# Joining two vector steps of a stick-breaking attention, and moving the loads of its output projection behind the last stores of keys

## The chip, the cores and the metric

The kernel runs on one core of one Trainium2 chip. The metric is the device time of one execution in microseconds (us), the median of several runs. The engines are named as the profile names them: PE (matrix multiply) with PEld (its weight loads), DVE (vector), ACT (scalar), POOL (GpSimd), SP (the queue that issues almost all of this kernel's DMAs).

## The reference

One layer of an encoder over 1024 frames of width 1024, in float32:

```python
h = rmsnorm(x, norm1_g)
qa, ka, va, qb, kb, vb = split(h @ w_in)          # 8 heads of 64 in group A, 8 in group B
ya = chunked_attention(qa, ka, va, rel_bias)      # softmax over 9 chunks of 64 keys
yb = stick_breaking_attention(qb, kb, vb)         # below
x = x + concat(rmsnorm(ya), rmsnorm(yb)) @ w_out
x = x + conv_gated_mlp(rmsnorm(x, norm2_g), ...)  # up 2*2816, causal conv of width 3, SiLU gate, down
return rmsnorm(x, final_g)
```

Stick-breaking attention of one head, for queries t and keys s < t, with z the scaled score: `a = exp(log_sigmoid(z) + suffix)`, where `suffix` is the sum of `log_sigmoid(z) - z` over the keys between s and t. In products: a key's weight is sigmoid(z) times the product of (1 - sigmoid(z)) over the keys between it and the query. If c is the running product of (1 - sigmoid(z)), each weight is the difference of two neighbours of c.

## The kernel before

**Stages.** Times from the profile: values and the projections of group B to about 171 us; stage B, the attention of group B, 176 to 329 us; stage A, the attention of group A, about 339 to 488 us; then the two halves of the output projection (`pb`, `pa`), the second norm and the channel mixer to the end. Time runs backwards in the kernel's arrays (frames are reversed), so that "later" keys of a query are a prefix in memory.

**Who sets the order.** The instruction order of every engine is fixed when the program is written, by a planner in the kernel (`Flow`). A piece of work is a `Chain` of steps, each with the engine it occupies (V, S, G, or D for the DMA queue), a cost from a small formula, and an action that emits the instruction. `flow.add` files a chain with the chains that it comes `after`; `flow.work(us)` moves the planner's clock on with the work of PE and emits every step that could have started by then, earliest first; of steps that could start at the same time the one with the smaller ready time plus `due` goes first. `load(kb, do)` costs `kb/260` us of D and lands 2.2 us later in the planner's eyes. The chip's own waits are semaphores on the data, put in by the framework; the planner decides only the order.

**Filler.** PE's order is: the attention's own products, and between them steps of a generator, `filler()`. A filler step is three matmuls of 128x512 and is counted as 0.68 us. First come the seven projections that group A needs (`project_qk`, tiles `q_p`, `k_p`, 112 steps), then the half of the output projection that belongs to group B (`out_b`, `out_part`, tile `pb`, 64 steps). `run(amount)` takes filler at a fixed rate: RATE_B over a head pair of group B, `RATES_A[p]` us over the eight blocks of head pair p of group A. `ready(*chains)` takes filler for as long as the chains it is given aren't done by the planner's clock; where the generator yields None (nothing to give) it stops, and the planner's clock jumps. `Banks.get` hands out a PSUM bank after `ready` on the bank's last users. `need(n)` draws filler until the projections of head pair n have been stored.

**Stage B.** A `BlockB` is a head pair n and a block i of 128 queries, 64 units of one head in all. `scores` makes z in a bank of 1024 columns (`bigs`, two banks), a chain then does the sigmoid on ACT (L979) and the running product on DVE (`tensor_tensor_scan`, L968, out of PSUM into an SBUF tile `acts`), and a second chain the subtraction of neighbours in `acts` (L974; only the 128 columns of the diagonal block, the other blocks use differences of the values `dv` instead). `turn` waits for that (`ready(self.chain[h])`), transposes `acts` on PE (L998, tile `tpb`), and `output` multiplies with the values (L1012). Unit b's scores are written before the turning of unit b-2. The subtraction is a chain of its own with `due = -2`; the bank counts as free (`mine`) after the scan.

**Stage A.** Blocks of 128 queries, for head pairs p = 0..3 (n = 4..7): scores (`sa`, L1062 and L1063), mask and maximum on DVE, exponential on ACT (L1090), transposes (`tpa`, L1122), copies on ACT (L1126), output (`yy`, L1145). For p, the tiles `qa..lb` of n = p + 4 are loaded from DRAM (`load_qk`, L857, twelve DMAs of 256 KB); the tiles of n and n + 2 share their slots.

**The loads of the output projection.** Group B's heads were normalised and stored to DRAM (`spill`, in `finish_b`, chains `spilled`). `prepare_b(i)` loads two tiles `yh[i]`, `yl[i]` (i = 4..7) of 1 MB in all, in two halves g (L1192); they take the places of the normalised input `hh`, `hl`, which `project_qk` reads to its last step. `out_part` needs for half g the tiles i = 4, 5, 6, 7 one after the other, a filler step each. `load_x2(d)` loads the residual (L1227) that a finished part is added to (L1219). The stores of the keys of n = 7 (`qk_kept[7]`, L838) come from the last projection.

The part of `filler` after the projections, and the chain that each half's load is put behind:

```python
            load_x2(0)
            load_x2(1)
            for i in range(4, 8):
                while not spilled[i - 4]:
                    yield None
                prepare_b(i)
...
                last = [yb_chains[i - 1, g]] if i > 4 else [x2_chains[g]]
                yb_chains[i, g] = flow.add(load(512, begin), after=[*spilled[i - 4], *last])
```

Of the kernel before, what the change touches and what calls it, by code (L numbers as in the profile page):

```python
# [39 lines left out]
BACK, BACK_STEP = 1.0, 0.6  # L40
BEHIND_V = {"V": 1.0, "S": 5.0, "D": 7.0}
RATE_B, LEAD_B = 10.0, 4.0
RATES_A, LEAD_A = (11.0, 13.0, 13.0, 13.0), 6.5
LAG = 0.25
START = 8.0
SLACK = 0.6
# [18 lines left out]
def r32(ap):  # L65
    return ap.bitcast(F32)
# [3 lines left out]
def tile_hybrid_block(  # L70
# [44 lines left out]
    def one(tag, name, dt=F32, shape=(P, T), pool=cp):  # L115
        return pool.tile(list(shape), dt, tag=tag, name=name)
# [33 lines left out]
    def rows(g):  # L150
        return slice(g * GW, (g + 1) * GW)

    def mm3(outs, wh, wl, sl, mh, ml, first, last, groups=(0, 1)):
        for i, (w, t) in enumerate(((wh, mh), (wh, ml), (wl, mh))):
            for o, g in zip(outs, groups):
                PE.matmul(  # L156
                    o, w[:, sl], t[:, rows(g)],
                    start=first and i == 0, stop=last and i == 2,
                )

    def cols(k):
        return slice(k * P, (k + 1) * P)
# [30 lines left out]
    def hpair(k, name, tags=None):  # L193
        th, tl = tags or (f"h{k}", f"l{k}")
        return one(th, f"{name}h{k}", F32R), one(tl, f"{name}l{k}", F32R)
# [5 lines left out]
    with tc.tile_pool(name="kp", bufs=2) as kp:  # L201
# [422 lines left out]
        def on_v(n, do, own="V"):  # L624
            return own, n / 960 + 0.075, 0.09, do

        def on_s(n, do):
            return "S", n / 1200 + 0.1, 0.1, do
# [4 lines left out]
        def load(kb, do, us=2.2):  # L633
            return "D", kb / 260, us, do
# [118 lines left out]
        flow, raw_chains = Flow(), {}  # L753
# [28 lines left out]
        def fetch(queue=w_ready, pool=wp, tags=("wh", "wl"), bufs=None):  # L782

            if not w_next:
                return
            if (w_next[0] in LATE_W) != (queue is w_late):
                w_missed.append(1)
                return
            name, t, loaded = w_next
            w_next.clear()  # L790

            def high():
                t["h"] = pool.tile([P, D], F32R, tag=tags[0], name=f"{name}_h", bufs=bufs)
                S.copy(t["h"], t["r"])  # L794

            def low(c, n, eng):
                if not c:
                    t["l"] = pool.tile([P, D], F32R, tag=tags[1], name=f"{name}_l", bufs=bufs)
                c = slice(c, c + n)
                sub(t["l"][:, c], t["r"][:, c], t["h"][:, c], eng)  # L800

            if name == LATE_W[1]:
                rest = [on_v(D, lambda: low(0, D, V), "VL")]
            else:
                rest = [on_g(PIECE, lambda c=c: low(c, PIECE, GP)) for c in range(0, D, PIECE)]
            c = flow.add(on_s(D, high), *rest, after=[loaded], slack=SLACK)
            c.due = DUE
            queue.append((t, c))
            load_next([c])
# [3 lines left out]
        def take(queue=w_ready):  # L813
            t, c = queue.popleft()
            flow.need(c)
            return t["h"], t["l"]
# [10 lines left out]
        qk_kept = {n: [] for n in range(8)}  # L827
# [50 lines left out]
        def project_qk(n):  # L878
            for what in ("q", "k") if n > 4 else ("k",):
                wh, wl = take()  # L880
                outs, mine = [None] * G, [None] * G
                steps = [(g, k) for g in range(G) for k in range(KT)]
                count = [0] * G
                for i, (g, k) in enumerate(steps):
                    if not count[g]:
                        for _ in range(PATIENCE):
                            if pjs.free():
                                break
                            yield None
                        outs[g], mine[g] = pjs.get(f"{what}{n}_p{g}")  # L890
                    count[g] += 1
                    last = count[g] == KT
                    mm3(outs[g : g + 1], wh, wl, cols(k), hh[k], hl[k], count[g] == 1, last, (g,))
                    flow.work(0.68)
                    if i == len(steps) - 1:
                        fetch()
                    if last:
                        mine[g].append(spill_qk(n, what, outs, g))
                    yield 0.68
# [32 lines left out]
        class BlockB:  # L932
# [14 lines left out]
            def scores(self, h):  # L947
                i, nk = self.i, self.nk
                qa, qb, ka, kb, la, lb = [qk_of[self.n][i] for i in range(6)]
                q, k, l = ((qa, ka, la), (qb, kb, lb))[h]  # L950
                z, mine = bigs.get(f"z{self.nm}_{h}")
                w = nk * P

                at, parts = {
                    1: (P, ((0, 2 * P, -P),)), 5: (192, ((192, 320, 0), (GW, 320, 320))),
                }.get(nk, (0, ((0, GW, 0), (GW, w - GW, GW)) if nk > 4 else ((0, w, 0),)))
                for o, n, k0 in parts:
                    ks = slice(i * P + k0, i * P + k0 + n)
                    PE.matmul(z[:, o : o + n], q[:, cols(i)], k[:, ks], start=True, stop=False)
                    PE.matmul(z[:, o : o + n], q[:, cols(i)], l[:, ks], start=False, stop=True)  # L960
                    flow.work(n / 1200 + 0.03)
                z = z[:, at : at + w]
                a = b_acts.pop(0)
                b_acts.append(a)
                self.a[h] = a

                def left():
                    V.tensor_tensor_scan(  # L968
                        out=a[:, :w], data0=z, data1=first[:, :w], initial=1.0, op0=ALU.mult,
                        op1=ALU.max,  # L970
                    )

                def steps():
                    V.tensor_tensor(  # L974
                        out=a[:, : P - 1], in0=a[:, : P - 1], in1=a[:, 1:P], op=ALU.subtract
                    )

                mine.append(flow.add(
                    on_s(w + 75, lambda: S.activation(z, z, AF.Sigmoid, scale=-1.0)),  # L979
                    on_v(2 * w + 100, left),  # L980
                ))
                self.chain[h] = flow.add(on_v(190, steps), after=mine)
                self.chain[h].due = -2.0

            def turn(self, h, mate):

# [166 lines left out]
        rb_of, sq_of, y_chains, x2_chains, yb_chains = {}, {}, {}, {}, {}  # L1153
# [32 lines left out]
        def prepare_b(i):  # L1186
            yh[i], yl[i] = hpair(i, "y")
            for g in range(G):

                def begin(r=rows(g)):  # L1190
                    for t, x in zip(spill[i - 4], (yh[i], yl[i])):
                        nc.sync.dma_start(r32(x[:, r]), t[:, r])  # L1192

                last = [yb_chains[i - 1, g]] if i > 4 else [x2_chains[g]]
                yb_chains[i, g] = flow.add(load(512, begin), after=[*spilled[i - 4], *last])

        def out_part(wh, wl, base, d, g, name):
            o, mine = pjs.get(f"{name}_{d}_{g}")
# [26 lines left out]
        def load_x2(d):  # L1225
            x2[d] = one(X2_TAGS[d], f"x2_{d}")
            x2_chains[d] = flow.add(load(512, lambda: nc.sync.dma_start(x2[d], xT[d])))  # L1227
# [165 lines left out]
        def filler():  # L1393
            for n in PLAIN:
                yield from project_qk(n)
            load_x2(0)
            load_x2(1)
            for i in range(4, 8):
                while not spilled[i - 4]:
                    yield None  # L1400
                prepare_b(i)
            while 4 not in rb_of or any(not c.done or c.t > flow.now for c in rb_of[4][1]):
                yield None
            yield from out_b(EARLY)
            while at["qk"] < 6:
                yield None
            yield from out_b((2,))

        fill = filler()
        done = [0.0]  # L1410

# [34 lines left out]
        spilled, summed = [None] * 4, [None] * 4  # L1446
# [47 lines left out]
        with stage("b"):  # L1494
# [11 lines left out]
            for b in range(len(items) + 3):  # L1506
                cur, h = items[b] if b < len(items) else (None, 0)
# [14 lines left out]
                if ending:  # L1522
# [4 lines left out]
                    yy, mine = meds.get(f"y{pair[0].nm}")  # L1527
# [17 lines left out]
                if 0 <= b - 2 < len(items):  # L1545
                    u, h = items[b - 2]
# [71 lines left out]
        for b in range(len(blocks) + 2):  # L1618
# [24 lines left out]
            if cur and cur.p == 3 and cur.i in (3, 4):  # L1643
                g = cur.i - 3
                ready(last_sum[2, g])
                rn_chains["a", g] = flow_totals(sq_of[0][:, rows(g)], f"na_{g}", rn3[:, 4 * g : 4 * g + 4])
            for h in range(2):
                if cur:
                    cur.scores(h)
                if ending and h == 0 and ending.i % 2:  # L1650
# [4 lines left out]
                    yy, mine = meds.get(f"yy{ending.p}_{ending.i}")  # L1655
# [119 lines left out]
    with stage("ffn"):  # L1775
# [449 lines left out]
        steps = {}  # L2225
# [130 lines left out]
        for f in range(3, NF):  # L2356
            if f + 2 < NF:
                load_up(f + 2)
            left = Left(f + 1) if f + 1 < NF else None
# [138 lines left out]
```

## Time and profile before

| | |
|---|---|
| median of 3 runs (lowest, highest) | 1212.7 us (1212.63, 1214.37) |
| the profiled execution | 1214.88 us, of which 1213.2 us lie between its first and last instruction |
| busy: PE, PEld | 1192.5 us (98%), 985.0 us (81%) |
| busy: DVE, ACT, POOL | 927.6 us (76%), 681.9 us (56%), 157.4 us (13%) |
| granted PE clock | 0.996 of full speed |
| DMA | 166.92 MB, 138 GB/s on average |

Busy time of an engine is the union of its instructions' times; what is left of the span is its idle time, and for each idle stretch the profile names the instruction on another engine (or the DMA) whose end came last before the engine went on. PE is busy nearly throughout, so idle time of PE is what this kernel can still lose or win by its order. A granted clock of 1 in a stretch means that PE was not throttled there.

### The profile page before, as it was taken

Reading aid. Unit: us, or ns where it says so; the run is one execution under the profiler, and the core shown is the slowest. Engines: PE = TensorE matmul, PEld = TensorE weight load, DVE = VectorE, ACT = ScalarE, POOL = GpSimd, SP = SyncE. Lnnn points to the kernel's source line nnn. Section 1 sums busy time; section 2 is a strip of 40 time slices with the busy share of each in tenths; the row PEclk is TensorE's granted clock in tenths of the full one; section 3 lists DMA queues with packets and bytes.
Section 4 is the critical chain, followed back from the end, with each engine's and each line's share of the span. In section 5 each row is a group of like instructions: output and inputs, shape, how many; then the busy total and the mean of one; then the engine's idle time right before and its main releaser. Section 6 shows DMA issues by size and latency. Waiting matters only on the chain.

```text
span 1213.2 us, 17081 instructions
## 1 busy us (share of the span) xinstructions
PE 1192.5 (98%) x6268; PEld 985.0 (81%) x6268; DVE 927.6 (76%) x1383; ACT 681.9 (56%) x1251; POOL 157.4 (13%) x161
## 2 busy tenths in 40 slices
PE   9999999999999899999999999999999999999997
PEld 7788888888888678888878888888888888888886
DVE  7957748878766666459997877768777789979885
ACT  7865336666667766334665555555555555444435
POOL 0001031002211210332000000000000023132035
PEclk9999999999999999999999999999999999999998
DMA  9468686777377841243033222232222295520003
GB/s 331 135 209 264 192 244 182 204 184 196 123 205 188 241 111 53 87 143 120 35 104 105 71 86 89 69 105 70 87 87 70 88 367 239 193 85 1 1 1 139
DMA packets 73793, 166.92 MB, mean 138 GB/s; under 512 B 7783, under 2 KB 23271, under 8 KB 73710
## 3 DMA queue, kind: packets, MB, share of 16 engines
q1 hardware_dynamic: 73566, 165.79, 43.3%
q8 instruction: 49, 0.80, 0.3%
q14 instruction: 34, 0.28, 0.1%
q10 hardware_dynamic: 144, 0.05, 0.0%
HBM read 118.60 MB, written 47.20 MB: 137 GB/s over the span
## 4 chain that ended last, share of the span: by engine, by line
PE 68%; DVE 5%; ACT 2%; DMA 1%; issue 1%; SPq 0%; DVEq 0%; ACTq 0%
PE u_c L1895 9%; PE u_e L1895 9%; PE u_a L1895 9%; PE dz L2411 8%; PE u_b L1895 5%; PE dj L2411 4%; PE dm L2411 4%; PE pb L156 4%; PE pa L156 3%; PE yy L1145 2%; PE tpa L1122 2%; PE k_p L156 2%; PE q_p L156 2%; PE dnl L2331 1%; PE sa L1062 1%; PE sa L1063 1%
## 5 line engine op out<-in xcount | busy, mean ns | idle before, releaser
L968 DVE TENSOR_TENSOR_SCAN acts<-zb,first 128x128 f32<-128x128 f32 (+7 forms) x64 | 85.1, 1348 | 25.2 <-ACT zb L979 25.1
L1919 DVE SCALAR_TENSOR_TENSOR vt<-cv,taps,vt 128x1023 f32<-128x1023 f32 (+1 forms) x44 | 58.2, 1322 | 2.2 <-ACT vt L1913 1.4
L1919 DVE SCALAR_TENSOR_TENSOR gt<-cg,taps,gt 128x1023 f32<-128x1023 f32 (+1 forms) x44 | 56.4, 1281 | 0.9 <-ACT gt L1913 0.2
L1090 ACT ACTIVATE pa<-sa,sta 128x640 f32<-128x640 f32 (+4 forms) x64 | 43.1, 673 | 21.3 <-DVE sta L1081 10.3
L134 POOL TENSOR_TENSOR dx_0wl<-dr,dx_0wh 128x512 fp32r<-128x512 f32 x1 | 1.4, 1370 | 412.4 <-ACT dx_0wh L2162 412.4
L1002 ACT COPY tb<-tpb 128x128 f32<-128x128 f32 (+3 forms) x96 | 43.3, 485 | 16.2 <-PE tpb L998 15.7
L979 ACT ACTIVATE zb<-zb 128x128 f32<-128x128 f32 (+7 forms) x64 | 41.3, 645 | 17.5 <-PE zb L960 17.1
L1913 ACT ACTIVATE gt<-cg,cst,taps 128x1024 f32<-128x1024 f32 x22 | 27.4, 1245 | 37.0 <-DVE cg L1787 37.0
L998 PE MATMUL tpb<-ident,acts 128*128 128x128 f32 x288 | 43.8, 279 | 1.3 <-DVE acts L974 0.8
L1126 ACT COPY pta<-tpa 128x512 f32<-128x512 f32 (+3 forms) x80 | 36.8, 486 | 11.2 <-PE tpa L1122 11.0
L1081 DVE TENSOR_REDUCE sta<-sa 128x1 f32<-128x640 f32 (+4 forms) x64 | 41.9, 655 | 1.2
L998 PEld LDWEIGHTS tpb<-ident,acts 128*128 128x128 f32 x288 | 33.0, 140 | 11.9 <-issue 3.9
L1122 PE MATMUL tpa<-ident,pa 128*128 128x128 f32 x240 | 38.1, 278 | 3.8 <-ACT pta L1126 2.4
L1784 DVE TENSOR_TENSOR up_r<-up_r 128x512 f32<-128x512 f32 x60 | 41.2, 687 | 0.8
L1122 PEld LDWEIGHTS tpa<-ident,pa 128*128 128x128 f32 x240 | 27.6, 140 | 11.9 <-ACT pta L1126 4.8
L1078 DVE TENSOR_TENSOR sa<-sa,bias 128x256 f32<-128x256 f32 (+1 forms) x64 | 26.4, 413 | 11.3 <-PE sa L1063 8.2
L2083 ACT COPY u_b<-u_a 128x512 f32<-128x512 f32 x19 | 10.8, 571 | 38.1 <-PE u_a L1895 38.1
L1145 PE MATMUL yy<-pta,v 128*64 128x256 f32 (+1 forms) x288 | 29.7, 349 | 0.0
L1012 PE MATMUL yb<-tb,dv 128*64 128x128 f32 x448 | 29.5, 273 | 0.0
L1784 DVE TENSOR_TENSOR dr<-dr,dr 128x512 f32<-128x512 f32 x40 | 28.9, 741 | 0.0
L1707 POOL TENSOR_TENSOR n_acc<-n_acc,n_sq 128x384 f32<-128x384 f32 (+2 forms) x23 | 24.1, 1049 | 29.0 <-ACT n_sq L1706 28.3
L134 POOL TENSOR_TENSOR wo_l<-wo_r,wo_h 128x256 fp32r<-128x256 f32 x28 | 19.7, 736 | 62.4 <-ACT wo_h L794 62.4
(1403 smaller groups left out, 4012.5 us busy)
## 6 DMA issues: line engine op xcount, KB each, us to landing
up_r<-in_w_up_dram SPq DMA_DIRECT2D x44, 512.0 KB, 3.6
act<-vt SPq DMA_DIRECT2D x22, 512.0 KB, 2.6
dr<-in_w_dn_dram SPq DMA_DIRECT2D x20, 512.0 KB, 6.8
dr<-act SPq DMA_DIRECT2D x20, 512.0 KB, 7.9
wv<-in_w_v_dram SPq DMA_DIRECT2D x16, 256.0 KB, 5.4
xin<-in_xT_dram SPq DMA_DIRECT2D x16, 256.0 KB, 5.4
row<-in_x_rows_dram SPq DMA_DIRECT2D x16, 256.0 KB, 2.7
raw<-in_w_in_dram SPq DMA_DIRECT2D x8, 512.0 KB, 5.1
```

The costliest lines, as they stand in the source:

```text
L156: PE.matmul(o, w[:, sl], t[:, rows(g)], start=first and i == 0, stop=last and i == 2,)
L968: V.tensor_tensor_scan(out=a[:, :w], data0=z, data1=first[:, :w], initial=1.0, op0=ALU.mult, op1=ALU.max,)
L998: PE.transpose(tp[:, cols(b)], self.a[h][:, cols(b0 + b)], ident)
L1002: mine.append(flow.add(on_s(m * P, lambda o=o, tp=tp: S.copy(o, tp))))
L1081: V.tensor_reduce(out=st[:, h : h + 1], in_=full, axis=AX.XY if nk == 5 else AX.X, op=ALU.max, negate=True,)
L1090: on_s(w + 170, lambda: S.activation(po, full, AF.Exp, bias=st[:, h : h + 1], accum_out=st[:, 2 + h : 3 + h])),
L1122: PE.transpose(tp[:, cols(b)], self.pr[src][:, cols(c)], ident)
L1145: PE.matmul(yy[HS[h], q], v[:, c * P + h * 64 : c * P + (h + 1) * 64], t[:, h], start=j == 0, stop=j == len(parts) - 1, skip_group_check=True,
L1784: eng.tensor_tensor(out=out, in0=a, in1=b, op=ALU.subtract)
L1895: PE.matmul(o, w[:, cols(k)], t, start=start and k == 0 and i == 0, stop=k == 3 and i == 2, skip_group_check=True,)
L1919: V.scalar_tensor_tensor(out=t[:, : T - lag], in0=o[:, lag:], scalar=c1(c + ct), in1=t[:, : T - lag], op0=ALU.mult, op1=ALU.add,)
L2411: PE.matmul(o[m], w[:, cols(m)], t, start=i in (0, 1, 4, 5) and p == ps_[0] and j == 0, stop=p == ps_[-1] and j == 2, skip_group_check=True,)
```

## The change

Three edits.

1. In `BlockB.scores` the scan and the subtraction become one step of one chain, emitted back to back on DVE, with a cost of `2w + 270` elements in place of `2w + 100` and, in a chain of its own, `190`. The chain that `turn` waits for and the chain that frees the bank are now the same: the planner counts the bank as used until the subtraction is done.
2. In `filler`, after the projections, the generator yields None until the stores of group B's last head pair and of the keys of n = 7 have been emitted. Then all four `prepare_b` are called at once, and `load_x2(0)`, `load_x2(1)` after them. A half's load no longer comes after the half before it.
3. `RATES_A` becomes (11, 13, 10, 11).

No instruction is added or removed; the order and the places change.

```diff
-RATES_A, LEAD_A = (11.0, 13.0, 13.0, 13.0), 6.5
+RATES_A, LEAD_A = (11.0, 13.0, 10.0, 11.0), 6.5
...
                         out=a[:, :w], data0=z, data1=first[:, :w], initial=1.0, op0=ALU.mult,
                         op1=ALU.max,
                     )
-
-                def steps():
                     V.tensor_tensor(
                         out=a[:, : P - 1], in0=a[:, : P - 1], in1=a[:, 1:P], op=ALU.subtract
                     )
 
-                mine.append(flow.add(
+                self.chain[h] = flow.add(
                     on_s(w + 75, lambda: S.activation(z, z, AF.Sigmoid, scale=-1.0)),
-                    on_v(2 * w + 100, left),
-                ))
-                self.chain[h] = flow.add(on_v(190, steps), after=mine)
-                self.chain[h].due = -2.0
+                    on_v(2 * w + 70 + 200, left),
+                )
+                mine.append(self.chain[h])
...
-                last = [yb_chains[i - 1, g]] if i > 4 else [x2_chains[g]]
-                yb_chains[i, g] = flow.add(load(512, begin), after=[*spilled[i - 4], *last])
+                yb_chains[i, g] = flow.add(load(512, begin), after=spilled[i - 4])
...
+            while not spilled[3] or not all(c.done for c in (*spilled[3], *qk_kept[7])):
+                yield None
+            for i in range(4, 8):
+                prepare_b(i)
             load_x2(0)
             load_x2(1)
-            for i in range(4, 8):
-                while not spilled[i - 4]:
-                    yield None
-                prepare_b(i)
```

## The prediction

> **What bounds the kernel now.** First the busy times of the page, then the stretches of the stages, then the instructions of PE one by one where PE is idle, then the queue of SP in that stretch.
>
> ```profile
> PE 1192.5 (98%) x6268; PEld 985.0 (81%) x6268; DVE 927.6 (76%) x1383; ACT 681.9 (56%) x1251; POOL 157.4 (13%) x161
> ```
> ```profile
> core 0: us, PE busy (x) PEld busy (x) DVE busy (x) ACT busy (x) POOL busy (x), PEclk, DMA share, GB/s
> 176.00:329.50 153.50, 151.94 (x1255) 126.62 (x1253) 122.43 (x159) 96.71 (x195) 19.97 (x25) 1.00 0.69 183
> 345.00:394.20 49.20, 49.13 (x340) 40.18 (x341) 33.42 (x85) 36.61 (x96) 3.93 (x8) 1.00 0.82 202
> 394.20:406.50 12.30, 9.02 (x70) 6.55 (x68) 7.74 (x19) 9.62 (x24) 3.55 (x6) 1.00 0.99 317
> 406.50:429.00 22.50, 18.84 (x137) 14.16 (x136) 15.39 (x41) 16.09 (x46) 2.86 (x4) 1.00 0.88 200
> 429.00:450.00 21.00, 21.00 (x139) 17.08 (x139) 13.41 (x33) 13.58 (x40) 1.29 (x1) 1.00 0.43 108
> 450.00:488.00 38.00, 37.98 (x265) 31.02 (x264) 26.18 (x65) 26.31 (x69) 5.38 (x7) 1.00 0.12 43
> 488.00:510.70 22.70, 22.70 (x113) 18.59 (x112) 11.24 (x18) 6.64 (x10) 7.18 (x11) 1.00 0.31 102
> ```
>
> PE bounds nearly everything: whatever order the work is in, its 1192.5 us stay, and a change of order can win only idle time. In stage B (first stretch) that is 153.50 - 151.94 = 1.56 us. In stage A it is 3.28 us from 394.2 to 406.5 and 3.66 us from 406.5 to 429, together 6.94, and next to nothing before (0.07) and behind (0.02). So there is one hole, 35 us long. The rows of PE in it, with the last filler step of the projections (`k_p`) and the first of the output projection (`pb`):
>
> ```profile
> 393.95 0.39 PE L156 MATMUL k_p<-hTh,k_l 128*128 128x512 f32 x1
> ...
> 397.29 0.66 PE L1122 MATMUL tpa<-ident,pa 128*128 128x128 f32 x4 [1.82 <-ACT pta L1126]
> ...
> 405.91 0.39 PE L1062 MATMUL sa<-kb,qb 128*128 128x256 f32 x1 [1.03 <-ACT pa L1090]
> ...
> 406.50 0.48 PE L156 MATMUL pb<-yh,wo_h 128*128 128x512 f32 x1
> ...
> 410.54 0.44 PE L1122 MATMUL tpa<-ident,pa 128*128 128x128 f32 x2 [0.28 <-ACT pta L1126]
> ...
> 414.12 0.41 PE L1062 MATMUL sa<-ka,qa 128*128 128x320 f32 x1 [1.34 <-ACT pa L1090]
> ...
> 417.57 0.48 PE L156 MATMUL pb<-yh,wo_h 128*128 128x512 f32 x1
> ...
> 419.79 0.48 PE L156 MATMUL pb<-yh,wo_h 128*128 128x512 f32 x1
> ...
> 428.86 0.44 PE L1122 MATMUL tpa<-ident,pa 128*128 128x128 f32 x2 [1.23 <-DVE yq L1574]
> 429.05 0.48 PE L156 MATMUL pb<-yh,wo_h 128*128 128x512 f32 x1
> ```
>
> The releasers are links of the softmax chain, which are there at all times; elsewhere filler covers them. Here there is none: three single `pb` steps at 406.5, 417.6 and 419.8 in 35 us, and from the fourth, at 429.05, a steady flow and no idle time. The four steps are those that need tiles i = 4, 5, 6 and 7. The queue of SP says why they come so far apart:
>
> ```profile
> 387.78 1.31 SPq L1227 DMA_DIRECT2D x<-in_xT_dram  x2
> ...
> 396.63 0.33 SPq L838 DMA_DIRECT2D k_d<-k_f  x1
> 397.05 0.50 SPq L1192 DMA_DIRECT2D yh<-spill  x1
> ...
> 401.69 0.62 SPq L1192 DMA_DIRECT2D yl<-spill  x1
> 407.80 0.45 SPq L857 DMA_DIRECT2D qa<-q_d  x1
> ...
> 410.79 0.57 SPq L1192 DMA_DIRECT2D yh<-spill  x1
> ...
> 421.27 0.32 SPq L1192 DMA_DIRECT2D yl<-spill  x1
> ...
> 428.30 0.45 SPq L857 DMA_DIRECT2D lb<-k_d  x1
> ```
> ```profile
> SPq L857 <- PE sa L1063: 7.4, 2, 5.4
> ```
>
> Eight of the sixteen loads of `yh`, `yl` go out from 397.05 to 401.69, already behind the last store of keys. The other eight follow from 410.79 to 421.27, because the loads for head pair 3 (`qa`..`lb`) stand between and in front: the first of them waits up to 5.4 us for PE to leave the slot, and SP with it.
>
> **The loads (edit 2).** Nothing is added; what moves is the place of 16 loads of `y` and two of `x2` in SP's queue. The chain from half to half goes, and both `x2` go behind. The loads are filed when the projections end, those of head pair 3 only with its turn, some 14 us later; the planner prefers the one that is ready earlier, so all sixteen stand in front of `qa`. They start where they do now (the keys' store at 396.63 is in front of them already, so the new wait for that store costs nothing; it is hidden because no filler could run before the tiles are there). The planner takes 512/260 = 1.97 us for a half and 2.2 us to land, halves of g = 0 and 1 in turn: tiles 4 to 7 of g = 0 are there 4.2, 8.1, 12.0 and 16.0 us after a start at about 397, so it puts the steps at about 403 (behind the transposes and outputs already due), 406, 410 and 414 in place of 406.5, 417.6, 419.8 and 429. The data would be there: the second eight, 2.1 MB, take 6.6 us at the 317 GB/s of the third stretch and 10.5 us at the 200 of the fourth, so the last are issued by about 412 at the slowest, and the one that the fourth step needs earlier.
>
> From 414 on filler flows. Of the 3.66 us of the fourth stretch, 0.28 (at 410.54) and 1.34 (at 414.12) lie before that, and two steps of 0.69 us (below) fall among them: about 0.6 stays and 3.0 go. Of the 3.28 of the third stretch the 1.82 at 397.29 stays, since no tile is there; of the 1.03 at 405.91 the first step takes about half. Term: -3.5 us. Ends: 0, where the steps fall beside the gaps, and -6.94, where all idle time went. The `x2` loads end about 4 us later than the last `y`; they are first used by the addition behind the fourth step, and the bank it frees is wanted eight steps later: no cost, and if that cover were gone the 2 x 512 KB at 200 GB/s cost 5 us.
>
> What is late next is head pair 3's twelve loads, behind 1 MB of `x2` now.
>
> ```profile
> 447.93 0.39 PE L1062 MATMUL sa<-ka,qa 128*128 128x320 f32 x1
> ```
>
> This is its first use. Today's last load goes out at 428.30; the 1 MB adds 5 us at 200 GB/s, and the 9 us that SP's pause (401.69 to 410.79) leaves unused come back. About 435 against a use at 444 or later: nothing. The Trainium skill, "DMA: Bandwidth & Descriptors", section "Queues, rings and completion order", says that each DMA engine consumes one ring's descriptors in order, which speaks against putting 5 MB in front of the keys; the order of the rows above agrees, and by that rule alone the keys would still be early.
>
> **The rates (edit 3).** Head pairs 2 and 3 get 10 and 11 us of filler for 13 and 13: 5 us move behind stage A, where the filler runs without a gap:
>
> ```profile
> 504.26 2.75 PE pb L156 x12
> ```
>
> That is four steps, 0.69 us each. PE does the same work there, so moving costs nothing unless thinner filler opens gaps. The nearest row is the stretch 345 to 394.2, mostly head pair 0 at 11 us: 0.07 us idle. `ready` also draws filler beyond the rate where a chain is late. Term: +0.3 us; ends 0 and +5 (all that is moved becomes idle time).
>
> **Scan and subtraction (edit 1).** The same 128 instructions of DVE. Rows of the group, and one place where another scan stood between:
>
> ```profile
> L968 DVE TENSOR_TENSOR_SCAN acts<-zb,first x64: 396/1340/2292, 176.7 to 323.0; 128x128 f32<-128x128 f32 x8, 128x1024 f32<-128x1024 f32 x8, 128x256 f32<-128x256 f32 x8, 128x896 f32<-128x896 f32 x8
> L974 DVE TENSOR_TENSOR acts<-acts x64: 257/283/2209, 177.1 to 324.3; 128x127 f32<-128x127 f32 x64
> ```
> ```profile
> 274.27 2.59 DVE L968 TENSOR_TENSOR_SCAN acts<-zb,first 128x768 f32<-128x768 f32 x2
> 276.78 2.18 DVE L974 TENSOR_TENSOR acts<-acts 128x127 f32<-128x127 f32 x2
> ```
> ```profile
> 278.91 0.85 PE L998 MATMUL tpb<-ident,acts 128*128 128x128 f32 x6 [0.64 <-DVE acts L974]
> ...
> 280.22 0.55 PE L998 MATMUL tpb<-ident,acts 128*128 128x128 f32 x3
> ...
> 285.39 0.74 PE L998 MATMUL tpb<-ident,acts 128*128 128x128 f32 x5 [0.19 <-DVE acts L974]
> ```
>
> Two scans, then their two subtractions, and the first unit's transposes wait 0.64 us. Joined, the first subtraction ends a scan earlier and that wait and the 0.19 go: -0.8. The second unit's scan starts 0.28 us later; its transposes (280.22) come 1.26 us after their subtraction ends (276.78 + 2.18 = 278.96), so that is covered; without that cover 32 such pairs cost 32 x 0.28 = 9 us. The bank is really free after the scan (the subtraction doesn't touch it); only the planner holds it 0.28 us longer and puts a filler step earlier instead: +0.3. Term: -0.5; ends -1.56 (all idle time of the stage) and +9, and I stay near the first, because DVE is busy 122.43 of 153.5 us there and PE does not wait for it otherwise. The Trainium skill, "VectorE: DVE Perf Modes", section "Rules for kernel authors", says that fusing chained vector operations gains nothing, only fewer of them do. The median of 283 ns agrees, for DVE's own time; by the rule the term is 0 and the sum -3.2.
>
> **Sum.** -3.5 + 0.3 - 0.5 = -3.7 us. The profiled execution took 1214.88 us (span 1213.2), 2.2 us over the median of 1212.7: 1211.2 for such an execution, 1209.0 for the median.
>
> **Rivals.** What a measurement can tell from no change is about 0.2%, 2.4 us.
>
> *Nothing gained.* The hole is a stretch without filler because the tiles can't be loaded before the projections end; its gaps at 397 and 405 lie before any tile, and if steps fall beside the gaps the term is -1 and the sum -1: 1212. For it: half of the idle time has such a place. Against: the gaps at 414 and 428.86 lie behind the tiles' new times.
>
> *Slower: thin filler.* In head pairs 2 and 3 the 5 us taken away become idle time: -3.5 + 5 - 0.5 = +1, and with no gain from the loads +4.5: 1214 to 1217. It decides once over 3.7 us of the 5 turn idle. For it: without filler the hole has 6.94 us idle in 34.8. Against: the 0.07 above.
>
> *Slower: the second scan.* If the later second scan of a pair is what the turning waits for, it costs up to 9 us, 1217; it decides from 13 of the 32 pairs on. Against: the 1.26 us above.
>
> *Keys late.* If SP's order moves head pair 3's loads past 444, each us counts; at 10 us late 1219. Against: 9 us in hand.
>
> **How the numbers follow.** Forecast 0.55 (1206 to 1210.3; its own range comes from a hole closed by 2.4 to 6.9 us), nothing gained 0.25 (1210.3 to 1215), thin filler 0.10, second scan 0.07, keys 0.03. Faster 0.55, same 0.25, slower 0.20. The range reaches from 1205.5 (hole closed, stage B's idle gone) to 1216 (into the thin filler) and leaves out about 0.15.
>
> **What would show it.** All sixteen `yh`, `yl` loads in one run on SP from 397 to about 410, `qa` behind them; four `pb` steps before 416 and steady ones behind; idle time of PE in the hole down from 6.94 to about 3.4; idle below 1 us in head pairs 2 and 3; more `pb` steps after the last `yy`; no scan between a scan and its subtraction, and PE's waits for `acts` down from 0.8. I am wrong if the `y` loads are split by `qa` again, if PE waits for a DMA at a `pb` step, or if the idle time shows up again between 430 and 485.

## The result, and the profile after

The changed kernel takes 1210.93 us (median of 14 runs), the kernel before in the same session 1212.99 us (14 runs). The ratio is 0.9982, with a 95% interval of 0.9974 to 0.9990: 0.18% faster, about 2.1 us. The forecast was 1209.0, in a range from 1205.5 to 1216.

Executions of one and the same kernel take some 1.4 us longer where their granted clock is 0.995 or 0.996 than where it is 0.997 or 0.998, and two took two to three times as long as all others (one of the changed kernel's 14, 2421 us, and the profiled one of `e_before` below, 3455 us), so times that are set against each other below are medians over executions at 0.997 or 0.998: 1212.9 for the kernel before (59 executions beside the experiments) and 1210.7 for the changed one (9), a difference of 2.2 us. The profiled execution of before had 0.996, that of the changed kernel (1210.40 us, span 1208.7) 0.998.

First the busy times of the changed kernel, and the same stretches as before:

```profile
PE 1189.4 (98%) x6268; PEld 984.7 (81%) x6268; DVE 932.1 (77%) x1383; ACT 682.3 (56%) x1251; POOL 157.1 (13%) x161
```
```profile
core 0: us, PE busy (x) PEld busy (x) DVE busy (x) ACT busy (x) POOL busy (x), PEclk, DMA share, GB/s
176.00:329.50 153.50, 151.37 (x1262) 129.28 (x1261) 126.28 (x158) 98.80 (x198) 20.18 (x25) 1.00 0.69 186
345.00:394.20 49.20, 48.64 (x336) 39.29 (x334) 33.49 (x85) 36.00 (x96) 4.68 (x10) 1.00 0.76 189
394.20:406.50 12.30, 9.70 (x71) 6.98 (x73) 7.88 (x20) 10.31 (x28) 4.07 (x5) 1.00 0.91 297
406.50:429.00 22.50, 21.02 (x150) 17.19 (x147) 16.02 (x41) 15.29 (x41) 1.35 (x2) 1.00 1.04 276
429.00:450.00 21.00, 20.52 (x140) 15.97 (x141) 15.20 (x40) 14.87 (x45) 4.32 (x7) 1.00 0.17 49
450.00:488.00 38.00, 37.88 (x263) 30.47 (x260) 24.77 (x61) 25.26 (x67) 4.09 (x5) 1.00 0.21 76
```

Two things stand out. From 345 to 429 PE is idle for 0.56 + 2.60 + 1.48 = 4.6 us, where it was idle for 0.07 + 3.28 + 3.66 = 7.0 us; behind 429 it is idle for 0.48 + 0.12 = 0.6 us, where there was 0.02. And PE's busy time, of the same 6268 instructions, fell by 3.1 us, which a mere change of order was not supposed to do. In stage B (first stretch) idle time even rose, from 1.56 to 2.13 us.

SP's queue, with the last stores of keys (`k_d`), the first and the last of the sixteen loads, and what follows them:

```profile
394.86 0.33 SPq L838 DMA_DIRECT2D k_d<-k_f  x1
395.28 0.41 SPq L1189 DMA_DIRECT2D yh<-spill  x1
...
404.90 0.32 SPq L1189 DMA_DIRECT2D yl<-spill  x1
405.56 1.01 SPq L1223 DMA_DIRECT2D x<-in_xT_dram  x2
...
407.73 0.45 SPq L857 DMA_DIRECT2D qa<-q_d  x1
...
422.22 0.45 SPq L857 DMA_DIRECT2D lb<-k_d  x1
```

All sixteen stand in one run from 395.28 to 404.90, where before the second eight went out from 410.79 to 421.27. The last load of head pair 3 goes out at 422.22 instead of 428.30. PE in the same place, its idle stretches and the `pb` steps:

```profile
392.18 0.39 PE L156 MATMUL k_p<-hTh,k_l 128*128 128x512 f32 x1
...
395.52 0.66 PE L1119 MATMUL tpa<-ident,pa 128*128 128x128 f32 x4 [1.82 <-ACT pta L1123]
...
402.87 0.47 PE L156 MATMUL pb<-yh,wo_h 128*128 128x512 f32 x1
...
404.14 0.39 PE L1059 MATMUL sa<-kb,qb 128*128 128x256 f32 x1 [0.33 <-ACT pa L1087]
...
405.49 0.38 PE L1059 MATMUL sa<-ka,qa 128*128 128x256 f32 x1 [0.52 <-ACT pa L1087]
...
408.32 0.39 PE L156 MATMUL pb<-yh,wo_h 128*128 128x512 f32 x1
...
412.55 0.41 PE L1059 MATMUL sa<-ka,qa 128*128 128x320 f32 x1 [1.36 <-ACT pa L1087]
...
416.01 0.48 PE L156 MATMUL pb<-yh,wo_h 128*128 128x512 f32 x1
...
416.79 0.39 PE L156 MATMUL pb<-yh,wo_h 128*128 128x512 f32 x1
...
417.48 0.39 PE L156 MATMUL pb<-yh,wo_h 128*128 128x512 f32 x1
```

The hole, from the last `k_p` step to the fourth `pb` step, is 24.6 us long instead of 35.1. Its steps came at 402.9, 408.3, 416.0 and 416.8. No `pb` step waits for a DMA.

### The profile page after: what moved, and what is told of

Read it like the earlier page. It is cut to its first block, busy times and chain, and to the rows that moved or that the text cites. A ratio compares the mean times of both kernels' runs of the same rounds, so it can differ in the third digit from the quotient of the medians.

```text
span 1208.7 us, 17078 instructions
## 1 busy us (share of the span) xinstructions
PE 1189.4 (98%) x6268; PEld 984.7 (81%) x6268; DVE 932.1 (77%) x1383; ACT 682.3 (56%) x1251; POOL 157.1 (13%) x161
## 4 chain that ended last, share of the span: by engine, by line
PE 87%; DVE 8%; ACT 3%; issue 1%; DMA 0%; POOL 0%; DVEq 0%; SPq 0%; ACTq 0%; POOLq 0%
PE u_c L1891 9%; PE u_e L1891 9%; PE u_a L1891 9%; PE dz L2407 8%; PE u_b L1891 5%; PE dj L2407 4%; PE dm L2407 4%; PE pb L156 3%; PE pa L156 3%; PE k_p L156 3%; PE v_x L510 3%; PE q_p L156 2%; PE yy L1142 2%; PE v_y L510 2%; PE tpa L1119 2%; PE tpb L995 2%
```

## The experiments

The theory: the loads close the hole and win most of what is won, the join a little, the rates nothing. The rivals: the gain comes from one edit alone; the edits undo each other; the join costs or wins by the bank and not by its order. The table gives, for each profiled execution, the length in us of the stages on PE, counted from start to start of instructions (B: first `zb` to the first `sa` of stage A; hole as above; rest: to the last `yy` of stage A; tail: to the last `pb`, with the number of its steps; pa: to the last `pa`). "Stages" is the sum of the columns and of the head pairs of stage A ahead of the hole (54.3 to 54.4, but 55.1 in `e_bank`), less that of the kernel before (380.4). "Time" is the difference of the medians at the higher clock, and the last column is the ratio of all runs, the two long ones left out, with its interval.

Five profiles have the same order of PE in stage B, that of before, and there B is 162.8, 162.9, 163.0, 163.4 (`e_tail`) and 163.7 (before itself); the table takes 162.9 for before, near the middle one. With its own 163.7 every other kernel would stand 0.8 lower in "stages", which the times don't bear out.

| kernel | B | hole | rest | tail (steps) | pa | stages | time | ratio |
|---|---|---|---|---|---|---|---|---|
| before | 162.9 (163.66 in its own profile) | 35.10 | 60.38 | 21.06 (28) | 46.57 | 0 | 0 | |
| changed | 161.99 | 24.61 | 69.02 | 21.04 (28) | 46.83 | -2.6 | -2.2 | 0.9982 (0.9974 to 0.9990) |
| e_scan | 162.03 | 35.10 | 60.39 | 21.06 (28) | 46.57 | -0.9 | -1.0 | 0.9989 (0.9980 to 0.9998) |
| e_loads | 162.80 | 24.60 | 72.41 | 16.51 (22) | 48.43 | -1.3 | -1.5 | 0.9986 (0.9977 to 0.9995) |
| e_rates | 162.94 | 35.09 | 60.18 | 22.78 (30) | 46.56 | +1.5 | +2.2 | 1.0013 (1.0004 to 1.0022) |
| e_noscan | 163.00 | 24.62 | 69.05 | 21.04 (28) | 47.05 | -1.3 | -1.3 | 0.9984 (0.9975 to 0.9993) |
| e_bank | 162.59 | 35.08 | 60.41 | 21.08 (28) | 46.66 | +0.5 | +0.5 | 1.0001 (0.9992 to 1.0010) |
| e_join | 162.05 | 24.61 | 69.34 | 21.04 (28) | 46.96 | -2.1 | -1.9 | 0.9984 (0.9975 to 0.9994) |
| e_tail | 163.44 | 35.11 | 64.44 | 16.53 (22) | 49.11 | +2.6 | +2.0 | 1.0013 (1.0004 to 1.0022) |
| e_halves | 161.95 | 17.68 | 77.54 | 16.49 (22) | 48.43 | -4.0 | -4.0 | 0.9963 (0.9951 to 0.9976) |
| e_halves_thin | 161.98 | 17.69 | 75.17 | 18.35 (24) | 46.58 | -6.3 | -6.4 | 0.9942 (0.9929 to 0.9954) |
| e_both | 160.82 | 17.57 | 75.44 | 19.04 (25) | 46.55 | -6.6 | -6.6 | 0.9943 (0.9931 to 0.9956) |
| e_pieces | 160.74 | 17.68 | 75.38 | 18.31 (24) | 46.64 | -7.3 | -7.3 | 0.9944 (0.9931 to 0.9958) |

The sums of stages and the times agree within 0.4 us in all rows but two (`e_rates` 0.7, `e_tail` 0.6): what is won and lost lies in these stages. The second norm and the channel mixer behind them are unchanged code; their 654.7 to 656.3 us go with the clock, 656.0 and more in the four profiles at 0.995 or 0.996 and 655.3 or less in the nine others. In all thirteen the clock is 1 from stage B up to the last 15 us, so the stages of the table are not touched by it.

**The kernel before once more** (no edit), as the measure of what a comparison can tell:

> The kernel before once more, for a second profile. The changed kernel was 2.06 us faster in the medians, but its profiled span is 4.5 us shorter, and 3.35 us of that lie between the first scores of group B and the last product of pa. Theory A (the three edits changed only those stages, the rest is scatter of the profiled execution): the stretch from the first scores to the last pa is 381.1 us again within 0.3, stage B 163.7, and the rest of the span is shorter by about 1 us than in the first profile. Theory B (stage B itself scatters from execution to execution by more than a microsecond, so the 1.67 us that it lost after the change prove nothing): stage B comes out between 162 and 163. Time: 1212.99, ratio 1.000.

Its ratio is 0.9998 (0.9989 to 1.0007): differences under 0.1% can't be told by ratios alone, and the stages in the profile have to tell them. Its profile is of the execution of 3455 us and can't decide what it was taken for, whether stage B scatters. The five profiles above do: it scatters by 0.9 us in the order of before. The PE instructions are the same, and the lengths differ behind one place, where DVE waits for a DMA of `spill`, a store of group B's finished heads:

```profile
231.76 0.75 DVE L1461 SCALAR_TENSOR_TENSOR yb<-y,cst,yb 128x512 fp32r<-128x512 f32 x1 [1.50 <-DMA spill<-yb]
```

That is before. In `e_tail`, `e_noscan`, `e_rates` and `e_loads` the same row waits 1.33, 0.93, 0.68 and 0.46 us, in the order of their B (163.4, 163.0, 162.9, 162.8); from PE's scores at about 233 and 239 on, the stage runs later where the wait was longer (by 0.65 us in before against `e_noscan`). The kernels with the join have no wait in this row, and their B is 161.95 to 162.05 in five profiles (those with POOL's work in pieces, further below, are shorter still).

**Each edit alone, and two together.** `e_scan` is edit 1 alone, `e_loads` edit 2, `e_rates` edit 3 (their parts of the diff above), `e_noscan` edits 2 and 3.

> Edit 1 alone (scan and subtraction as one step). Theory A (joining takes away waits of transposes for their subtraction, which the profile hides partly because a matmul counts as busy for 0.39 us while the next starts after 0.23): stage B about 162.0 us as in the changed kernel against 163.7, the hole in stage A with 6.9 us of idle time as before; in all -1.7 us, 1211.3. Theory B (the gain of stage B is scatter, the rule that fusing gains nothing): stage B 163.7 and 1213.0. Theory C (the bank counted as used for longer costs): over 164.5 in stage B, 1214.

> Edit 2 alone (the loads behind the stores of keys, all at once). Theory A (the hole in stage A lasts as long as the filler lacks its tiles): the hole from the last projection step to the fourth pb step is 25 us long in place of 35, its idle time about 4.6 in place of 6.9, idle time behind it under 0.1 with the full rates; stage B unchanged at 163.7. In all -2.3 us, 1210.7. Theory B (the loads were hidden anyway and the whole gain came from stage B): the hole is shorter, its idle time turns up elsewhere, 1212.5 to 1213.

> Edit 3 alone (less filler in head pairs 2 and 3). Theory A (thinner filler opens small gaps behind the hole): idle time behind the hole about 0.6 in place of 0.02, hole unchanged, more pb steps after the last yy (about 33 in place of 28): +0.5 us, 1213.5. Theory B (filler is drawn on demand, a lower rate only moves it): 1213.0.

> The changed kernel without edit 1 (edits 2 and 3 alone). Theory A (edits 2 and 3 only work together, and edit 1 adds its part of stage B): stage B 162.8, the hole 24.6 us, 28 steps left, pa 46.8; +0.85 on the changed kernel, 1211.8. Theory B (edit 1 has no part in it): 1210.9.

The join is worth about 0.9 us wherever it stands: B is 162.0 with it and 162.8 to 163.7 without, and by time it wins 1.0 on the kernel before (`e_scan`) and 0.8 between `e_noscan` and the changed kernel. The loads alone win 1.3, although the hole closes by the full 10.5 us. Of that, 1.9 us come back in the output projection of group A (pa, 46.57 to 48.43). Its waits, in `e_loads` and (further below) `e_tail`; columns are total, number, longest:

```profile
PE pa L156 <- ACT wo_h L794: 0.7, 1, 0.7
```

PE waits there for the cast of a weight tile (`wo_h`). Filler that is given out earlier is missing behind the last `yy`: 22 steps instead of 28, and the casts for `pa` had run beside these steps. The rates put the six steps back (28) and pa is 47.0 again, but thinner filler lengthens rest and tail by 69.05 + 21.04 - 72.41 - 16.51 = 1.2 us. Edit 3 beside edit 2 is therefore 1.2 - 1.4 = -0.2 by these stages, nothing that the times show. Alone it has no wait to remove (28 steps were enough) and costs 1.5 by the stages and 2.2 in time, more than either theory of its expectation; the other 0.7 lie in none of the stages.

**Is the tail of filler the cover?** If the missing steps are the cause, filler given out earlier must cost the same with the loads of before:

```diff
-RATES_A, LEAD_A = (11.0, 13.0, 13.0, 13.0), 6.5
+RATES_A, LEAD_A = (11.0, 13.0, 13.0, 17.0), 6.5
```

> The kernel before with one rate raised: 17 in place of 13 us of filler in head pair 3, so that about 22 pb steps are left behind the last yy in place of 28. Loads and their order as before. In the run of edit 2 alone, and in that of the halves in another order, 22 steps were left and pa took 48.4 us in place of 46.6, with 0.7 us of PE waiting for the cast of a weight. Theory A (these steps are the cover under which the weights of pa are loaded, cast and split; edit 3 is there to keep them): pa 48.4 us and the same wait, all else as before, +1.8 us, 1214.7. Theory B (the longer pa comes from the moved loads): pa 46.6, 1213.

```profile
PE pa L156 <- ACT wo_h L794: 1.3, 1, 1.3
```

With 22 steps behind the last `yy` the wait is there without any moved load, and pa is 49.1 us. (Of the +2.6 in the table 0.5 is its longer B; rest, tail and pa together cost 2.1.) Moving filler forward is no free move: the last 24 steps or so are the cover of the next weights (24 keep pa at 46.6 in `e_halves_thin`).

**What of the join wins: its order, or the bank that is held longer?** `e_bank` is before with the bank counted as used until the subtraction; `e_join` is the changed kernel with the bank counted as free 0.2 us earlier.

```diff
 # e_bank, on the kernel before
                 self.chain[h].due = -2.0
+                mine[:] = [self.chain[h]]
 # e_join, on the changed kernel; Sooner passes on a chain's state with its time less 0.2
-                mine.append(self.chain[h])
+                mine.append(Sooner(self.chain[h], 0.2))
```

> The kernel before, but a bank of scores counts as free only after the subtraction, which stays a step of its own. In the run of edit 1 alone, stage B took 162.0 us against 162.8 to 162.9 in the two runs without edit 1, and the filler stood in other places: 46 times straight before scores and 7 times before transposes, against 26 and 19. Theory A (the late bank does it: the planner draws filler before the scores, where it gives the subtraction time): about 46 and 7 here too, stage B near 162.0, 1212.0. Theory B (the join does it, by taking other scans out from between): 26 and 19 about as before, stage B 162.8 or longer, 1213.0.

> The changed kernel, but the planner counts a bank of scores as free 0.2 us before the joined step ends, about when the scan itself ends. Theory A (late bank): filler back before the transposes, stage B 162.8, in all +0.8 on the changed kernel, 1211.8. Theory B (join): stage B 162.0, 1210.9.

With the bank alone B is 162.59, 0.2 below the shortest in the order of before, and 0.7 us are lost in the head pairs ahead of the hole (55.06 instead of 54.37). With the bank back, the join keeps B at 162.05. So it is the join. How much of its gain is the wait for `spill` that goes with it, no run separates. But it doesn't win by the waits that the prediction named. The rows of `acts` in the changed kernel (minimum, median and maximum in ns), and stage B of `e_noscan`, whose clock is the same:

```profile
L968 DVE TENSOR_TENSOR_SCAN acts<-zb,first x64: 415/1350/2291, 176.6 to 321.3; 128x128 f32<-128x128 f32 x8, 128x1024 f32<-128x1024 f32 x8, 128x256 f32<-128x256 f32 x8, 128x896 f32<-128x896 f32 x8
L972 DVE TENSOR_TENSOR acts<-acts x64: 290/292/2354, 177.1 to 322.6; 128x127 f32<-128x127 f32 x64
```
```profile
PE tpb L995 <- DVE acts L972: 1.3, 1, 1.3
```
```profile
176.00:329.50 153.50, 152.14 (x1258) 127.20 (x1257) 122.60 (x159) 97.12 (x197) 19.99 (x25) 1.00 0.70 183
```

Three short waits of transposes for `acts` (1.1 us together) became one of 1.3 us, the next scores wait twice for a scan (0.9 us together, none in `e_noscan`), idle time in the stage rose from 1.36 to 2.13, and still the stage is 1.0 us shorter: PE's busy time holds hidden waits. Two matmuls of 512 columns that wait for nothing start 0.23 us apart (391.04 and 391.27 in the trace of the changed kernel), while each has a duration of 0.39: a matmul that comes up to 0.16 us late shows no gap. Counted from start to start, less the smallest interval behind a filler matmul in the stage, transposes right behind a filler step lost about 1.0 us at 19 places in `e_noscan` and lose 0.15 at 7 in the changed kernel, since the joined order puts filler ahead of the scores (46 places for 26) and not ahead of the transposes. The scores behind filler lose in turn, 0.8 us for 0.2, so 0.3 of these two stays as gain. Other successions change in both directions; how the 1.0 us divides further stays open.

The Trainium skill, "Perfetto Trace Analysis", section "Identifying the Most-Contended Engine", says that matmul busy share is no good measure of how close a kernel is to its roofline, because pipelined instructions look smaller in the trace. These runs agree that it is no measure: 2.2 us of busy time went between `e_noscan` (1191.6) and the changed kernel (1189.4), 1.8 of them in stage B, with the same 6268 matmuls and the same clock of 0.998. They don't show it by that reason: a row here is longer (0.39 us) than the step to the next matmul (0.23).

**The loads in the order in which the steps need them.** The planner gives halves 0 and 1 in turn; `out_part` needs the four tiles of half 0 first.

```diff
             for i in range(4, 8):
-                prepare_b(i)
+                prepare_b(i, 0)
             load_x2(0)
             load_x2(1)
+            for i in range(4, 8):
+                prepare_b(i, 1)
```

`e_halves_thin` has RATES_A (11, 13, 8, 11) beside it, so that filler is left behind stage A.

> The changed kernel with the loads in another order: the four halves g = 0 first, then the residuals, then the four halves g = 1. In the changed kernel the hole (last projection step to fourth pb step) is 24.6 us with 4.6 us of idle time, 1.36 of it in one piece, 18 us in. Theory A (the hole lasts until the fourth tile is there by the planner's clock, 4.2 + 3 x 1.97 = 10.1 us after the loads' start in place of 16): hole about 17 us, idle time about 3.2 (the 1.36 covered), and 28 pb steps or a few fewer behind the last yy; -1.4 us on the changed kernel, 1209.5. Theory B (more filler early leaves too little behind stage A, as in the run of edit 2 alone, where 22 steps were left, pa took 48.4 us for 46.6 and PE waited for its weights): fewer than 25 steps behind, pa over 47.5 us, 1211.

> The same with RATES_A (11, 13, 8, 11), so that the steps drawn early are kept back later. Theory A: hole as in the run before it, 28 steps or more behind the last yy, pa 46.7 us, idle time behind the hole 0.6 to 1: 1209.5 or just below. Theory B (thin filler opens gaps): idle time behind the hole over 1.5, 1211.

PE in the hole of `e_halves`:

```profile
395.60 0.66 PE L1119 MATMUL tpa<-ident,pa 128*128 128x128 f32 x4 [1.82 <-ACT pta L1123]
...
397.81 0.44 PE L1059 MATMUL sa<-ka,qa 128*128 128x384 f32 x1 [0.43 <-ACT pa L1087]
...
402.94 0.48 PE L156 MATMUL pb<-yh,wo_h 128*128 128x512 f32 x1
...
404.22 0.39 PE L1059 MATMUL sa<-kb,qb 128*128 128x256 f32 x1 [0.33 <-ACT pa L1087]
...
404.81 0.48 PE L156 MATMUL pb<-yh,wo_h 128*128 128x512 f32 x1
...
408.40 0.40 PE L156 MATMUL pb<-yh,wo_h 128*128 128x512 f32 x1
...
409.94 0.48 PE L156 MATMUL pb<-yh,wo_h 128*128 128x512 f32 x1
```

The steps come at 402.9, 404.8, 408.4 and 409.9, and the gaps of 0.52 and 1.36 us are gone: the idle time in the hole is 2.6 us. So the late third step of the changed kernel (416.0) was a matter of the order of halves. It was the planner's doing and not that of the chip's transfers: in the trace of the changed kernel one of the two loads for the third step, issued at 399.12, has landed at 405.54, and one of those for the fourth at 408.74, 10 and 8 us before the steps. Alone, this falls into the trap of the tail again (22 steps, pa 48.43); with thinner filler pa is 46.58 and the kernel is 6.4 us faster than before. That is 3 us more than was expected. Against the changed kernel the stages are 3.7 us shorter, and idle time gives 2.6 of them (2.0 in the hole, and 0.04 for 0.60 behind it); the rest stays open.

**The two largest waits that were left.** `e_both` is `e_halves_thin` with two edits: POOL's addition of squares in `finish_b` in four pieces of 256 columns, and the cast ahead of the wait of 1.82 us on ACT put 3 us later. `e_pieces` has the first alone.

```diff
-                ops.append(on_g(T, lambda: GP.tensor_tensor(out=yb_of[0], in0=yb_of[0], in1=y, op=ALU.add)))
+                ops += [
+                    on_g(PIECE, lambda o=yb_of[0][:, c : c + PIECE], x=y[:, c : c + PIECE]: plus(o, o, x, GP))
+                    for c in range(0, T, PIECE)
+                ]
 # e_both alone, where a weight's cast is filed
+            if name == "wo1":
+                c.t += 3.0
```

> The last and fastest of the runs before this (halves in another order, rate 8 in head pair 2), with two more edits that act in different stages. First, POOL's addition of squares in stage B in four pieces of 256 columns: in all profiles a subtraction that meets POOL's addition of 1024 columns (2.4 us) takes 2.0 to 2.4 us in place of 0.28 and ends 0.15 us behind it, and PE then waits 1.26 us at 275. Theory A (the two share a way to their memory and the vector instruction waits for the other's end): the longest subtraction below 0.9 us, that wait gone, stage B about 161.0 in place of 162.0. Theory B (the subtraction was late for other reasons): stage B 162.0. Second, the cast of the output projection's second weight (1.03 us on ACT, at the start of the hole) planned 3 us later, because it stands in front of the copies of transposes for which PE waits 1.82 us. Theory A: that wait below 0.9, hole 16.7 in place of 17.7. Theory B (the wait is that of the softmax chain itself): hole 17.7. Both A: 1204.5; both B: 1206.5.

> The run before without its second edit: halves in another order, rate 8 in head pair 2, POOL's addition of squares in four pieces. In the run before, stage B fell from 162.0 to 160.8 us, but from the last projection step to the last pb step it took 112.05 us for 111.2, and the time was the same within its scatter. Theory A (the pieces give 1.2 us, the later cast takes 0.8 back by moving the idle time to the next scores): stage B 160.8, hole to last pb 111.2, 1205.4. Theory B (the pieces themselves cost later on): hole to last pb 112, 1206.3.

The reason for the first edit is in these rows of the changed kernel, one of DVE, one of POOL and one of PE:

```profile
273.91 2.35 DVE L972 TENSOR_TENSOR acts<-acts 128x127 f32<-128x127 f32 x1
```
```profile
273.74 2.37 POOL L1487 TENSOR_TENSOR y<-y,y 128x1024 f32<-128x1024 f32 x1 [18.49 <-ACT y L1485]
```
```profile
276.41 0.85 PE L995 MATMUL tpb<-ident,acts 128*128 128x128 f32 x6 [1.26 <-DVE acts L972]
```

The subtraction takes 0.29 us in the median and 2.35 here: it ends 0.15 us after POOL's addition, and the transposes wait 1.26 us. In `e_pieces` the longest subtraction is 0.89 us and B is 160.7 instead of 162.0:

```profile
L972 DVE TENSOR_TENSOR acts<-acts x64: 290/292/892, 177.3 to 321.6; 128x127 f32<-128x127 f32 x64
```

At one clock `e_pieces` is 0.9 us faster than `e_halves_thin` (1205.6 and 1206.5; two and four executions), as the stages say; the medians over all runs (1206.70 and 1206.48) don't show it, because three of its five executions had the lower clock. The ratio is the same as that of `e_halves_thin`, so this last step rests on the stages and these few executions. The later cast won nothing: in `e_both` the wait of 1.82 became one of 0.88 and one of 1.14, and from the hole to the last `pb` it takes 112.05 us where `e_pieces` takes 111.37.

`e_halves_thin`, `e_both` and `e_pieces` beat both kernels, by 0.6% against the kernel before.

## Why the prediction was right or wrong

*The loads, -3.5.* The mechanism held: one run of loads, `qa` behind them, the first step at 402.9 for 403, the flow of filler from 416.8 on. The size was off. Idle time in the hole fell by 2.4 us, the low end of the forecast's own range, because the second, third and fourth steps came at 408.3, 416.0 and 416.8 and not at 406, 410 and 414, so that two and not four stood before 416. Those were the planner's earliest times; its next places for filler lay later, on the other side of the gap of 1.36 us at 412.55, which the sum had half covered. The gap of 0.52 at 405.49 stayed as well. Idle time in the hole is 4.6 us where I expected 3.4.

*The rates, +0.3.* The size is near (-0.2 by the stages) by luck, since two effects that I didn't have cancel, and the working is wrong. I priced filler behind stage A as work that costs the same there; it is the cover under which the next weights are cast, and without edit 3 its loss costs 1.4 us. Thinner filler costs 1.2 in turn. Six steps moved (22 against 28), not four, and as the loads had drawn six more ahead, 28 are left behind the last `yy` as before, where I expected more.

*The join, -0.5.* It measured -0.9, and the step behind it fell: the transposes' waits for `acts` didn't go down from 0.8, they became one of 1.3, and the scores' waits for a scan rose from 0.3 to 0.9. The 0.3 for the bank didn't show (B 161.99 with it, 162.05 without). The joined order wins inside PE's busy time.

*"Its 1192.5 us stay."* This premise fell: busy time is 1191.6 without and 1189.4 with the join, at the same clock. The 1.56 us of idle time was therefore no bound for what stage B could win.

*The sum.* -2.4 (hole) + 0.6 (thinner filler) + 0.3 (pa) - 0.9 (join) is -2.4, beside -2.6 by the stages and -2.2 in time, where I had -3.7. The placing of the median 2.2 us under the profiled execution was right. Some 1.4 of it go with that execution's clock (0.996, for 0.997 or 0.998 in most), and its stage B was 0.7 us longer than the middle one of its order.

*The costs set at nothing.* Keys for head pair 3 and the `x2` loads behind the others cost nothing that the profile shows: the keys' last load went out earlier than before, and nothing waits for either.

*The rivals.* "Nothing gained" was wrong as a mechanism, since the hole closed; but the half of it that spoke for it, steps that fall beside gaps, is what made the gain small, and the measured 1210.9 lies just inside the 1210.3 to 1215 that I gave to it and outside the 1206 to 1210.3 of the forecast proper. That it lies in the whole range is owed to that range's width. The bound of 0.2% lies inside the measured interval of 0.10 to 0.26%. Thin filler was real at 0.6 us of idle time, far from the 3.7 at which it would have decided. The second scan did not decide: the waits for scans above are 0.9 us, and B got shorter wherever the join stood.

## What to carry to other kernels

Filler is not free to move: before it is given out earlier, look at what is loaded or cast beside it where it stands now, and leave enough of it there. When loads are moved ahead, file them in the order in which the consumer takes them; here that, with filler thinned to keep the cover, won another 4.2 us on the 2.2 of the change. And judge a change of order by the length of the stage from first to last instruction, not by the idle time in it.

## What the runs showed of the hardware that was not expected

- A subtraction on DVE with both inputs in SBUF was held until POOL's addition that had started before it was done: 2.35 us instead of 0.29, ending 0.15 us after it. In `e_bank` one that starts 1.49 us into the addition takes 1.06 us and ends 0.15 us after it too. The Trainium skill, "SBUF — State Buffer", section "Who interferes with whom", says that a DVE instruction with two SBUF inputs contends with a GpSimd instruction that reads SBUF; these rows agree, and with POOL's work in four pieces the longest is 0.89 us. The prediction had the row of 2.18 us in its quotes and read past it.
- PE's idle time and the length of a stage can move in opposite directions: 1.36 to 2.13 us idle, 163.0 to 162.0 us long.
- The lower mean clock of some executions is one short stretch near their end. In the four profiles at 0.995 or 0.996 PE runs at 0.5 of its clock for 3.4 us, beginning 14.0 to 14.6 us before the end (1199.1 to 1202.5 of 1213.2 in that of before), and again in the last 7.1 to 7.7; the nine profiles at 0.997 or 0.998 show only such an end, of 4.7 to 8.0 us. What sets off the first isn't shown.
